# RWKV-7 and mLSTM stages of a hybrid encoder layer: decay as diagonal matrices, state copies on ScalarE, coefficients by rows, products ordered by tile shape

## The chip, the core and the metric

The kernel runs on one core of a Trainium2 chip. The metric is the device time of one execution in microseconds. TensorE is called PE here, VectorE DVE, ScalarE ACT, GpSimd POOL, SyncE SP; SP, and sometimes ACT, only start DMAs.

## What is computed

One layer of an encoder with 1024 positions of width 1024, all in 32-bit floats. A normalised input is projected once to the inputs of four mixers (RWKV-7, mLSTM, RG-LRU, HGRN2) and to four gate blocks; the gated mixer outputs are projected back and a convolutional feed-forward network follows. The shift, scale and gate vectors come from `c` by a projection ("ada"). The change touches the first two mixers, in both directions of time, and the ada projection:

```python
# RWKV-7, 8 heads of 64; S is v x k
S_t = S_{t-1} diag(w_t) + (S_{t-1} a_t) b_t^T + v_t k_t^T ;  y_t = S_t r_t
k_bonus = 0.5 * (kts[0] + kts[1])
bonus = jnp.sum(r_h * k_bonus * r_k, axis=-1, keepdims=True) * v_h
y = (groupnorm(ys[0] + ys[1]) * ln_w + ln_b + bonus) * (sigmoid(xg) @ g2)
# mLSTM, 4 heads: decayed attention inside a chunk plus a matrix state between chunks
```

## The kernel before

Everything is written for one core, with positions in blocks of 128. A scheduler orders the instructions of each engine, by priorities and dependencies; in the RWKV loop PE's order is the order in the code (a manual schedule), and a few instructions are tied to come after a named one.

**The RWKV loop** (`rw_first`, `rw_btm`, `rw_solve`, `rw_second`, `rw_chain`, about L890 to L1165, driven from L1307) makes 16 turns, one for each pair of heads `j` and pair of blocks. A turn handles four chunks of 64 positions for each of two heads and two directions, and three groups of chunks are under way at once: the chain of one, the second half of the preparation of the next, the first half of the one behind that. The gate projections, some 1200 products of 128x512, fill PE between the steps (`pieces`).

- First half: DVE scans the log decays (L863), ACT takes two exps per direction (L865, L867), DVE and POOL build `rw_AR` and `rw_BK` (L877 to L885), PE multiplies them (L915), DVE masks the products (L923). Then 16x16 triangular blocks go through DRAM by DMAs on SP (L971 to L976), ACT copies them (L978) and DVE inverts them by small products and sums (L986 to L999): the solve.
- Second half: `rw_second` joins the small inverses to 64x64 ones in four stages (L1026, L1033, L1046, L1054). `rw_btm` turns `rw_BK` by PE transposes (L956) and copies it to `rw_btm` (L957, ACT).
- Chain: four steps, each L1117 (state `rw_mv` times keys), a copy `rw_s` (L1120, ACT), L1127 (times the inverse), a copy `rw_uv` (L1130, ACT), L1134 (old state by an identity) plus L1142 (update) into one PSUM tile, and L1148 (DVE), which multiplies that tile by the decay of the chunk `rw_gc` and writes the next state `rw_mv`, or `rw_M` behind the last step. The outputs are L1091 and L1096, in two places of the step.

**The epilogue** `rw_post` (L1165) makes 8 blocks of norm, bonus and gate on POOL, DVE and ACT, one product on PE (L1202) and four transposes (L1206). The bonus needs coefficients, one per head and position, that the loop makes with a two-column selector (L931) and ACT keeps (L934). HGRN2 and its projections run beside the epilogue.

**mLSTM** `ml_pair` (L575) makes two heads: state updates (L605, DVE L610), scores (L631), and for each head, direction and chunk the sum of two products, decayed scores times values (L643, contraction 128) and query times state (L644, contraction 64), three chunks to a PSUM bank, copied by ACT (L648). `fill` puts other projections in between. Beside it run sixteen ada pieces: 1 MB of weights each, summed into one tile by DVE (L1382, L1384) and one by POOL (L1391, L1395), then one-column products with ones on PE (L1408).

## Time and profile before

| | us |
|---|---|
| median of 3 runs | 2743.36 |
| lowest, highest | 2740.43, 2747.32 |
| the profiled execution | 2752.19 |
| its span, first to last instruction | 2750.4 |
| PE, DVE, POOL, ACT busy in it | 2539.7, 1781.4, 1178.2, 916.3 |

The order of the stages in the profiled execution: norm, ada and first projections to about 440 us, the RWKV loop to 1050, the epilogue of RWKV beside the projections of HGRN2 to 1180, HGRN2 to 1500, mLSTM to 1750, then branch outputs and feed-forward network. In the rows below times are microseconds from the start of the span, unless marked ns.

### The profile page before, as it was taken

To read this page: it belongs to the slowest core of one execution; us is meant where nothing else is said; L and a number is where in the kernel's file an instruction comes from. 1 tells how busy PE (TensorE), PEld (TensorE's weight loads), DVE (VectorE), ACT (ScalarE), POOL (GpSimd) and SP (SyncE) were. 2 spreads that over 40 slices of the span, in tenths; PEclk is the share of its full clock that TensorE was granted. 3 is DMA by queue.
4 is the path that set the end of the run, shared out by engine and by line. 5 is a ranking of instruction groups with operands and counts; after the bars stand their busy time and mean duration, and the time that the engine had idled before them with its cause. 6 is when DMAs were issued, how large, how long until landed. Compare 5 with 4: busy or idle time off the path is not lost. (4 is left out here: it accounts for less than half of the span.)

```text
span 2750.4 us, 46997 instructions
## 1 busy us (share of the span) xinstructions
PE 2539.7 (92%) x18625; PEld 2032.3 (74%) x18625; DVE 1781.4 (65%) x2868; ACT 916.3 (33%) x1653; POOL 1178.2 (43%) x1164
## 2 busy tenths in 40 slices
PE   5999888999999999799989999999998999999998
PEld 4777666676776777587778767788776888887887
DVE  7567765676667733754553675367479998896345
ACT  4355532333333322433332232111234444342002
POOL 3654462443344315632212443367456444445332
PEclk9999998999999999999989988999999999999999
DMA  6422253444444324311111544554542222216222
GB/s 214 130 70 65 89 153 79 115 108 111 105 106 113 95 72 132 88 44 41 47 32 36 154 132 140 184 189 156 174 121 88 92 83 79 85 57 202 83 80 77
DMA packets 402117, 290.25 MB, mean 106 GB/s; under 512 B 121258, under 2 KB 364248, under 8 KB 401896
## 3 DMA queue, kind: packets, MB, share of 16 engines
q1 hardware_dynamic: 362920, 247.85, 31.1%
q10 hardware_dynamic: 38976, 39.40, 4.3%
q8 instruction: 146, 2.39, 0.4%
q14 instruction: 75, 0.61, 0.1%
HBM read 223.40 MB, written 63.77 MB: 104 GB/s over the span
## 5 line engine op out<-in xcount | busy, mean ns | idle before, releaser
L119 POOL TENSOR_TENSOR w_lo<-w_raw,w_hi 128x512 fp32r<-128x512 f32 x284 | 393.2, 1385 | 780.9 <-DVE w_hi L118 277.7
L125 PE MATMUL pbig<-uh,w_hi 128*128 128x512 f32 x1208 | 508.2, 422 | 23.4 <-ACT w_hi L116 8.5
L127 PE MATMUL pbig<-uh,w_lo 128*128 128x512 f32 x1208 | 485.3, 403 | 6.7 <-POOL w_lo L119 6.6
L126 PE MATMUL pbig<-ul,w_hi 128*128 128x512 f32 x1184 | 477.0, 403 | 0.0
L125 PEld LDWEIGHTS pbig<-uh,w_hi 128*128 128x128 f32 x1208 | 233.3, 193 | 91.0 <-ACT gt L1230 17.4
L127 PEld LDWEIGHTS pbig<-uh,w_lo 128*128 128x128 f32 x1208 | 233.4, 194 | 62.0 <-POOL w_lo L119 10.8
L126 PEld LDWEIGHTS pbig<-ul,w_hi 128*128 128x128 f32 x1184 | 229.6, 194 | 42.0 <-issue 1.3
L118 DVE CAST w_hi<-w_raw 128x512 fp32r<-128x512 f32 x224 | 134.0, 599 | 144.9 <-PE pbig L126 82.6
L127 PE MATMUL ppc<-uh,w_lo 128*128 128x512 f32 x340 | 135.6, 402 | 2.6 <-POOL w_lo L119 2.2
L125 PE MATMUL ppc<-uh,w_hi 128*128 128x512 f32 x340 | 134.5, 400 | 1.2 <-DVE w_hi L118 1.2
L126 PE MATMUL ppc<-ul,w_hi 128*128 128x512 f32 x320 | 127.8, 400 | 0.0
L125 PE MATMUL ppa<-uh,w_hi 128*128 128x512 f32 x220 | 87.2, 397 | 5.5 <-DVE w_hi L118 5.4
L127 PE MATMUL ppa<-uh,w_lo 128*128 128x512 f32 x220 | 86.9, 395 | 0.8 <-POOL w_lo L119 0.8
L127 PE MATMUL ppy<-uh,w_lo 128*128 128x512 f32 x216 | 85.3, 395 | 1.1 <-POOL w_lo L119 1.1
L125 PE MATMUL ppy<-uh,w_hi 128*128 128x512 f32 x216 | 85.8, 397 | 0.1
L1833 ACT CAST w_hi<-s 128x512 fp32r<-128x512 f32 x84 | 52.1, 620 | 97.3 <-PE ppc L126 22.4
L126 PE MATMUL ppa<-ul,w_hi 128*128 128x512 f32 x208 | 84.1, 404 | 0.0
L126 PE MATMUL ppy<-ul,w_hi 128*128 128x512 f32 x208 | 82.7, 398 | 0.0
L127 PEld LDWEIGHTS ppc<-uh,w_lo 128*128 128x128 f32 x340 | 65.8, 194 | 17.9 <-POOL w_lo L119 2.6
L125 PEld LDWEIGHTS ppc<-uh,w_hi 128*128 128x128 f32 x340 | 65.3, 192 | 16.5 <-DVE w_hi L118 2.1
L1384 DVE SCALAR_TENSOR_TENSOR ada_acc<-ada_w,sc,ada_acc 128x256 f32<-128x256 f32 x112 | 73.1, 655 | 2.0
L204 ACT CAST uh<-h_raw 128x1024 fp32r<-128x1024 f32 x22 | 23.0, 1052 | 151.9 <-PE ppc L127 123.8
(789 smaller groups left out, 6319.1 us busy)
## 6 DMA issues: line engine op xcount, KB each, us to landing
w_raw<-in_w_in_dram SPq DMA_DIRECT2D x172, 256.0 KB
ada_w<-in_ada_w_dram SPq DMA_DIRECT2D x24, 1024.0 KB
s_raw<-in_ffn_up_dram SPq DMA_DIRECT2D x84, 256.0 KB
dG<-gt ACTq DMA_DIRECT2D x64, 256.0 KB
sgt<-dG SPq DMA_DIRECT2D x32, 512.0 KB
rw_in<-dIn SPq DMA_DIRECT2D x32, 384.0 KB
w_raw<-in_ffn_down_dram SPq DMA_DIRECT2D x44, 256.0 KB
dF<-cv SPq DMA_DIRECT2D x22, 512.0 KB
```

The lines of the kernel that those rows point to most:

```text
L118: nc.vector.tensor_copy(out=hi, in_=raw[:, k0:k0 + m])
L119: nc.gpsimd.tensor_tensor(lo, raw[:, k0:k0 + m], hi.bitcast(F32), op=SUB)
L125: nc.tensor.matmul(pt, lhsT=wh, rhs=uh, start=start, stop=False)
L126: nc.tensor.matmul(pt, lhsT=wh, rhs=ul, start=False, stop=False)
L127: nc.tensor.matmul(pt, lhsT=wl, rhs=uh, start=False, stop=stop)
L204: nc.scalar.copy(hi, src)
L1384: nc.vector.scalar_tensor_tensor(acc, w[:, k, :], self.sc[:, k:k + 1], acc, op0=MUL, op1=ADD)
L1833: nc.scalar.copy(hi, x)
```

## The change

1. **Chain.** For each turn POOL makes 64x64 diagonal matrices `dg` out of the decays (L960 of the new kernel). The old state is multiplied by them on PE (four products in place of two by an identity), and `rw_btm` is built as a product of `rw_BK` with `dg` in place of a transpose, so that the PSUM tile holds the decayed state at once. ACT copies it (L1153) where DVE multiplied it.
2. **Outputs.** The products for y of a step stand in one place, those of one tile shape together.
3. **Coefficients.** The selector becomes the weight and the data stream past it, which gives rows of 256 positions; ACT copies them, SP writes them to DRAM (`dC`), and the epilogue loads, adds and transposes them (L1183).
4. **Order of the loop.** The first three stages of `rw_second` move one place to the back; the solve stands in the code behind the first step of the next turn.
5. **mLSTM.** The two kinds of products are grouped by bank, two chunks to a bank, and `MF` and the rate of the filler follow. **ada**: POOL adds the two partial sums, so that PE makes one product where it made two.

```diff
@@ -568,7 +568,7 @@
     SEQ = "q0 p0 q1 a32 o0 p1 o1"
-    MF = (2, 1, 2)
+    MF = (2, 2, 2)
@@ -634,18 +634,21 @@
                 num = self.t(wp, [P, NCK, 129], f"ml_num{d}")
-                for g in range(0, NCK, 3):
-                    n = min(3, NCK - g)
-                    pt = self.ps([P, 512])
-                    for i in range(n):
-                        c = g + i
-                        o = pt[:, 129 * i:129 * i + 129]
-                        nc.tensor.matmul(o, lhsT=D[d][:, c, :], rhs=v[:, c, h, :], start=True, stop=False)
-                        mm = nc.tensor.matmul(o, lhsT=Qd[d][r, c * P:(c + 1) * P], rhs=St[d][r, c, :],
-                                              start=False, stop=True)
+                for gs in ((0, 2), (4, 6)):
+                    pts = [self.ps([P, 512]) for _ in gs]
+                    for i in range(2):
+                        for x in ((0, 1), (1, 0))[i]:
+                            for g, pt in zip(gs, pts):
+                                c, o = g + i, pt[:, 129 * i:129 * i + 129]
+                                l, rr = ((D[d][:, c, :], v[:, c, h, :]) if x == 0 else
+                                         (Qd[d][r, c * P:(c + 1) * P], St[d][r, c, :]))
+                                mm = nc.tensor.matmul(o, lhsT=l, rhs=rr, start=(x == i), stop=(x != i))
...
                     self.fill(mm, self.MF[1])
-                    nc.scalar.copy(num[:, g:g + n, :], pt[:, :129 * n].rearrange("p (n v) -> p n v", v=129))
+                    for g, pt in zip(gs, pts):
+                        nc.scalar.copy(num[:, g:g + 2, :], pt[:, :258].rearrange("p (n v) -> p n v", v=129))
@@ -700,11 +703,12 @@
             nc.gpsimd.memset(x, 0.0)
+        self.rw_e64 = self.t(wp, [P, 64], "rw_e64")
+        nc.vector.tensor_tensor(self.rw_e64, self.ident[:, 0:64], self.ident[:, 64:P], op=ADD)
...
         z = self.rw_TFt[0].rearrange("p d m t -> p (d m t)")
-        self.last_pm = None
@@ -925,13 +929,14 @@
             yield
-        pt = self.ps([P, 2, NB, 2], self.pat())
+        pt = self.ps([P, 2, P * NB], self.pat())
         for d in range(2):
-            for n in range(NB):
-                nc.tensor.matmul(pt[:, d, n, :], lhsT=ops[d][2][:, P * n:P * n + P], rhs=self.rw_sel[:, j, :],
-                                 start=True, stop=True)
+            nc.tensor.matmul(pt[0:2, d, :], lhsT=self.rw_sel[:, j, :], rhs=ops[d][2], start=True, stop=True)
         for d in range(2):
-            nc.scalar.copy(self.rw_coef[:, d, n0[d]:n0[d] + NB, 2 * j:2 * j + 2], pt[:, d])
+            cf = self.t(wp, [2, P * NB], "rw_tmp", bufs=3)
+            nc.scalar.copy(cf, pt[0:2, d, :])
+            nc.sync.dma_start(out=self.dC[2 * j:2 * j + 2, d, P * n0[d]:P * (n0[d] + NB)], in_=cf)
@@ -949,12 +954,20 @@
+        dg = b["dg"] = self.t(wp, [P, 2, NC, 64], "rw_dg", bufs=2)
+        nc.gpsimd.tensor_tensor(dg, self.rw_e64.unsqueeze(1).to_broadcast([P, 2 * NC, 64]).rearrange(
+            "p (d c) k -> p d c k", d=2), b["gc"].unsqueeze(3).to_broadcast([P, 2, NC, 64]), op=MUL)
+        pts = [self.ps([P, 2, NC, 64], self.pat()) for h in range(2)]
         for d in range(2):
-            bk = b["bk"][d]
-            pt = self.ps([P, NC, P], self.pat())
             for c in range(NC):
-                nc.tensor.transpose(pt[:, c, :], bk[:, c, :, :], self.ident)
-            nc.scalar.copy(btm[:, d], pt)
+                for h in range(2):
+                    hr = slice(64 * h, 64 * h + 64)
+                    nc.tensor.matmul(pts[h][:, d, c, :], lhsT=b["bk"][d][hr, c, :, :], rhs=dg[hr, d, c, :],
+                                     start=True, stop=True)
+        for h in range(2):
+            nc.scalar.copy(btm[:, :, :, 64 * h:64 * h + 64], pts[h])
@@ -1045,7 +1058,7 @@
                                  start=True, stop=True, tile_position=(32 * q0, 32 * q1))
-        E3 = self.t(wp, [P, NC, 32], "rw_E3")
+        E3 = self.t(wp, [P, NC, 32], "rw_E")
@@ -1079,28 +1092,21 @@
-        def y(st, part):
+        def y(st):
             cs = (st, NC - 1 - st)
-            if st % 2 == 0 and part == 0:
+            if st % 2 == 0:
...
-            def y2(d, start):
+            for d, c in enumerate(cs):
                 for h, hr, _ in halves:
-                    nc.tensor.matmul(py[hr, st % 2, d, :], lhsT=b["cb"][hr, d, cs[d], 64:P], rhs=b["uv"][hr, d, cs[d], h, :],
-                                     start=start, stop=not start, tile_position=(64 * h, 64 * h))
-            def y1(d, start):
+                    nc.tensor.matmul(py[hr, st % 2, d, :], lhsT=b["cb"][hr, d, c, 64:P], rhs=b["uv"][hr, d, c, h, :],
+                                     start=(d == 0), stop=True, tile_position=(64 * h, 64 * h), skip_group_check=True)
+            for d, c in enumerate(cs):
                 for h, hr, _ in halves:
-                    nc.tensor.matmul(py[hr, st % 2, d, :], lhsT=b["ar"][d][:, cs[d], 1, h, :], rhs=b["mv"][:, d, cs[d], h, :],
-                                     start=start, stop=not start, tile_position=(0, 64 * h))
-            if part == 0:
-                y2(0, True)
-                y1(0, False)
-                y1(1, True)
-                return
-            y2(1, False)
+                    nc.tensor.matmul(py[hr, st % 2, d, :], lhsT=b["ar"][d][:, c, 1, h, :], rhs=b["mv"][:, d, c, h, :],
+                                     start=False, stop=True, tile_position=(0, 64 * h), skip_group_check=True)
@@ -1114,9 +1120,10 @@
                     for h, hr, _ in halves:
-                        nc.tensor.matmul(pt[hr, d, :], lhsT=b["ar"][d][:, c, 0, h, :], rhs=b["mv"][:, d, c, h, :],
-                                         start=True, stop=True, tile_position=(0, 64 * h))
-                s = self.t(wp, [P, 2, 64], "rw_s", bufs=2)
+                        self.last_s = nc.tensor.matmul(pt[hr, d, :], lhsT=b["ar"][d][:, c, 0, h, :],
+                                                       rhs=b["mv"][:, d, c, h, :], start=True, stop=True,
+                                                       tile_position=(0, 64 * h))
+                s = self.t(wp, [P, 2, 64], "rw_s")
@@ -1130,27 +1137,22 @@
                 pm = self.ps([P, 2, 64], "pc")
-                for h, hr, _ in halves:
-                    nc.tensor.matmul(pm[hr], lhsT=self.ident[hr, hr], rhs=both(b["mv"], st, h, hr), start=True, stop=True,
-                                     tile_position=(64 * h, 64 * h))
+                for d, c in enumerate(cs):
+                    for h, hr, _ in halves:
+                        nc.tensor.matmul(pm[hr, d, :], lhsT=b["dg"][hr, d, c, :], rhs=b["mv"][hr, d, c, h, :],
+                                         start=(d == 0), stop=True, tile_position=(64 * h, 64 * h), skip_group_check=True)
             if st:
-                y(st - 1, 0)
+                y(st - 1)
...
                     for h, hr, _ in halves:
-                        self.last_pm = nc.tensor.matmul(pm[hr, d, :], lhsT=b["btm"][:, d, c, hr], rhs=b["uv"][:, d, c, h, :], start=False,
+                        nc.tensor.matmul(pm[hr, d, :], lhsT=b["btm"][:, d, c, hr], rhs=b["uv"][:, d, c, h, :], start=False,
...
                 for h, hr, _ in halves:
-                    g = b["gc"][hr, 0, st:st + 1]
-                    g = bass.AP(g.tensor, g.offset, [list(g.ap[0]), [2 * (NC - st) - 1, 2], [0, 64]])
-                    mo = M[j][hr, :, h, :] if st == NC - 1 else both(b["mv"], st + 1, h, hr)
-                    nc.vector.tensor_tensor(mo, pm[hr], g, op=MUL)
-            if st:
-                y(st - 1, 1)
+                    nc.scalar.copy(M[j][hr, :, h, :] if st == NC - 1 else both(b["mv"], st + 1, h, hr), pm[hr])
             if st == NC - 1:
-                y(st, 0)
-                y(st, 1)
+                y(st)
@@ -1173,7 +1175,13 @@
         coef = self.t(wp, [P, NT, 8], "ro_coef")
-        nc.vector.tensor_tensor(coef, self.rw_coef[:, 0], self.rw_coef[:, 1], op=ADD)
+        cf = self.t(wp, [8, 2, T], "ro_cf")
+        nc.sync.dma_start(out=cf, in_=self.dC)
+        nc.vector.tensor_tensor(cf[:, 0], cf[:, 0], cf[:, 1], op=ADD)
+        pt = self.ps([P, NT, 8], "pc")
+        for n in range(NT):
+            nc.tensor.transpose(pt[:, n, :], cf[:, 0, P * n:P * n + P], self.ident[:8, :8])
+        nc.scalar.copy(coef, pt)
@@ -1274,7 +1282,7 @@
         self.dSG = self.t(dr, [P, T], "dSG")
-        self.rw_coef = self.t(self.cp, [P, 2, NT, 8], "rw_coef")
+        self.dC = self.t(dr, [8, 2, T], "dC")
@@ -1314,7 +1322,10 @@
                     next(chn, None)
-                    if st > 1:
+                    if st == 0 and g > 0:
+                        with self.tc.issue_after(self.last_s.ins):
+                            next(pend, None)
+                    if st == 3:
@@ -1327,6 +1338,8 @@
                         next(fst, None)
+                        if st == 3:
+                            next(sec, None)
@@ -1341,8 +1354,7 @@
                             lin = self.rw_lin(*order[g + 2], wp)
-                        with self.tc.issue_after(self.last_pm.ins) if self.last_pm is not None else ExitStack():
-                            next(fst, None)
+                        pend = fst
@@ -1395,7 +1407,9 @@
             if pend is None:
-                self.ada_end([(g, accs)], "pa", G)
+                if ks < 8:
+                    nc.gpsimd.tensor_tensor(acc, acc, accs[0], op=ADD)
+                self.ada_end([(g, [acc])], "pa", G)
@@ -1640,7 +1654,7 @@
                         self.filler = self.gates(dG, g0, 32 - self.NE)
-                        self.rate = 8.0 * (32 - self.NE - g0) / (4 * self.MF[0] + 12 * self.MF[1] + 6 * self.MF[2])
+                        self.rate = 8.0 * (32 - self.NE - g0) / (4 * self.MF[0] + 8 * self.MF[1] + 6 * self.MF[2])
```

The new lines move the instructions of an engine as follows. First ACT in the first step of a turn: `rw_s`, `rw_uv` and `rw_mv` are the chain's, `rw_tmp` and `rw_l` belong to the exps of the next group. Before (L865 and L867 are the exps, L957 copies `rw_btm`):

```order
L865 ACTIVATE rw_l_1520_9673<-rw_tmp_9779 128x256
L957 COPY rw_btm_9761<-ppt_9762 128x512
L867 ACTIVATE rw_tmp_9779<-rw_tmp_9779 128x256
L957 COPY rw_btm_9761<-ppa_9768 128x512
L865 ACTIVATE rw_l_1523_9682<-rw_tmp_9804 128x256
L867 ACTIVATE rw_tmp_9804<-rw_tmp_9804 128x256
L1120 COPY rw_s_9861<-ppc_9856 128x128
```

No copy of the state stands among them. In the changed kernel (L869 and L871 are the exps, L970 copies `rw_btm`):

```order
L1137 COPY rw_uv_8911<-ppc_9450 64x2x64 x2
L869 ACTIVATE rw_l_1488_9384<-rw_tmp_9500 128x256
L871 ACTIVATE rw_tmp_9500<-rw_tmp_9500 128x256
L869 ACTIVATE rw_l_1491_9393<-rw_tmp_9525 128x256
L871 ACTIVATE rw_tmp_9525<-rw_tmp_9525 128x256
L970 COPY rw_btm_9472<-ppa_9475 128x8x64
L970 COPY rw_btm_9472<-ppt_9476 128x8x64
L1153 COPY rw_mv_8916<-ppc_9457 64x2x64 x2
L1127 COPY rw_s_9570<-ppc_9565 128x128
```

The copies of `rw_btm` stood among the exps; now they stand behind all four, and the copy of the state, which was DVE's, stands behind them. On DVE before, the state stood here, behind both scans (L863) in the first step of a turn:

```order
L863 SCALAR_TENSOR_TENSOR rw_tmp_9779<-rwrs_717,rw_l_1520_9673 128x256
L883 SCALAR_TENSOR_TENSOR rw_tmp_9792<-rw_l_1521_9675,rw_in_9776 128x256
L877 TENSOR_TENSOR rw_AR_9783<-rw_in_9776,rw_l_1520_9673 64x4x63
L879 TENSOR_TENSOR rw_AR_9783<-rw_in_9776,rw_l_1520_9673 64x4x64
L877 TENSOR_TENSOR rw_AR_9783<-rw_in_9776,rw_l_1520_9673 64x4x63
L879 TENSOR_TENSOR rw_AR_9783<-rw_in_9776,rw_l_1520_9673 64x4x64
L863 SCALAR_TENSOR_TENSOR rw_tmp_9804<-rwrs_717,rw_l_1523_9682 128x256
L1148 TENSOR_TENSOR rw_mv_9229<-ppc_9748,rw_gc_8717 64x2x64 x2
L885 SCALAR_TENSOR_TENSOR rw_BK_9784<-rw_tmp_9792,rw_tmp_9779 64x4x64 x2
```

That row is gone from DVE in the changed kernel; the rest stands there as before.

On PE in the epilogue, one of the eight blocks before (L1206 the transposes of a block, L1202 the product of the next, the rest projections of HGRN2's input):

```order
L126 MATMUL pbig_11880<-ul_24_94,w_hi_11875 128x512
L127 MATMUL pbig_11880<-uh_16_86,w_lo_11876 128x512
L1206 MATMUL ppc_11510<-ident_73,ro_y_1766_11484 128x128 x4
L1202 MATMUL ppc_11541<-ro_1754_11442,ro_sg_11446 128x512
L125 MATMUL pbig_11879<-uh_17_87,w_hi_11875 128x512
L126 MATMUL pbig_11879<-ul_25_95,w_hi_11875 128x512
L127 MATMUL pbig_11879<-uh_17_87,w_lo_11876 128x512
```

Projections stand on both sides of the block. From the end of the projections on in the changed kernel, where L1214 and L1210 are the same two, PE has:

```order
L125 MATMUL ppy_12150<-uh_18_88,w_hi_12145 128x512
L126 MATMUL ppy_12150<-ul_26_96,w_hi_12145 128x512
L127 MATMUL ppy_12150<-uh_18_88,w_lo_12146 128x512
L1214 MATMUL ppc_11810<-ident_73,ro_y_1808_11784 128x128 x4
L1210 MATMUL ppc_11841<-ro_1803_11764,ro_sg_11768 128x512
L1214 MATMUL ppc_11844<-ident_73,ro_y_1817_11818 128x128 x4
```

All eight blocks follow one another there in this way; before, 16 to 70 rows of other products stood between two of them. On PE in mLSTM, from the end of one bank to the next (`pps`, `ppt`) before:

```order
L643 MATMUL pps_15870<-ml_v_11726,ml_D_2371_15816 128x129
L644 MATMUL pps_15870<-ml_S_2352_15686,ml_q_2350_15682 128x129
L643 MATMUL ppt_15878<-ml_v_11726,ml_D_2371_15816 128x129
L644 MATMUL ppt_15878<-ml_S_2352_15686,ml_q_2350_15682 128x129
L643 MATMUL ppt_15878<-ml_v_11726,ml_D_2371_15816 128x129
```

The kinds alternate, within a bank and from one to the next. One bank in the changed kernel (L647 is both kinds, told apart by `ml_D` and `ml_S`), with the projections that follow:

```order
L647 MATMUL ppt_16095<-ml_v_12060,ml_D_2407_16046 128x129
L647 MATMUL ppt_16095<-ml_S_2396_15987,ml_q_2394_15983 128x129 x2
L647 MATMUL ppt_16095<-ml_v_12060,ml_D_2407_16046 128x129
L126 MATMUL pbig_16759<-ul_19_89,w_hi_16748 128x512
L127 MATMUL pbig_16759<-uh_11_81,w_lo_16749 128x512
```

A bank's two products with the state now stand side by side, between two with the decayed scores.

## Rows read from the trace of the kernel before

**Rows 1.** The page: engines' busy time; costliest group (busy, mean ns, idle, releaser).

```profile
PE 2539.7 (92%) x18625; PEld 2032.3 (74%) x18625; DVE 1781.4 (65%) x2868; ACT 916.3 (33%) x1653; POOL 1178.2 (43%) x1164
...
L119 POOL TENSOR_TENSOR w_lo<-w_raw,w_hi 128x512 fp32r<-128x512 f32 x284 | 393.2, 1385 | 780.9 <-DVE w_hi L118 277.7
```

**Rows 2.** Windows by stage: stretch, its us, busy us (instructions) per engine, PEclk, DMA, GB/s.

```profile
440.00:1050.00 610.00, 565.18 (x7663) 434.51 (x7663) 391.19 (x979) 207.92 (x565) 224.23 (x358) 0.97 0.40 101
1060.00:1180.00 120.00, 101.93 (x730) 78.59 (x729) 80.17 (x119) 47.19 (x65) 80.03 (x59) 0.94 0.38 107
1510.00:1750.00 240.00, 225.28 (x1096) 174.07 (x1094) 148.73 (x259) 65.10 (x136) 96.17 (x89) 0.89 0.45 140
1608.00:1636.00 28.00, 24.57 (x94) 18.30 (x94) 18.97 (x28) 13.42 (x28) 13.31 (x12) 0.52 0.39 128
```

**Rows 3.** Waits of PE, 440 to 1050: waiter, releaser, total us, times, longest.

```profile
PE ppc L1117 <- DVE rw_mv L1148: 28.7, 17, 3.1
```

**Rows 4.** Timeline of one turn: start us, duration us, engine, line, output<-inputs, count, wait.

```profile
758.16 0.67 DVE L863 TENSOR_TENSOR_SCAN rw_tmp<-rwrs,rw_l 128x256 f32<-128x256 bf16 x1
...
758.87 0.42 ACT L865 ACTIVATE rw_l<-rw_tmp 128x256 f32<-128x256 f32 x1 [2.96 <-DVE rw_tmp L863]
...
759.19 0.57 ACT L957 COPY rw_btm<-ppt 128x512 f32<-128x512 f32 x1
...
761.74 0.69 DVE L863 TENSOR_TENSOR_SCAN rw_tmp<-rwrs,rw_l 128x256 f32<-128x256 bf16 x1
...
762.46 0.61 DVE L1148 TENSOR_TENSOR rw_mv<-ppc,rw_gc 64x128 f32<-64x128 f32 x2
...
762.80 0.77 PE L1117 MATMUL ppc<-rw_mv,rw_AR 128*64 128x64 f32 x8 [2.83 <-DVE rw_mv L1148]
...
772.70 0.45 PE L1026 MATMUL pps<-rw_RT,rw_cb 32*32 32x32 f32 x32
...
772.98 0.48 PE L1026 MATMUL pps<-rw_R,rw_cb 32*32 32x32 f32 x32
...
776.84 0.27 PE L915 MATMUL ppt<-rw_AR,rw_BK 64*128 64x128 f32 x1
...
776.95 0.27 PE L915 MATMUL ppt<-rw_AR,rw_BK 64*128 64x128 f32 x1
...
786.00 0.62 ACT L978 COPY rw_SB<-rw_pr 32x256 f32<-32x256 f32 x1 [0.57 <-DMA rw_pr<-dA]
...
795.92 0.68 DVE L863 TENSOR_TENSOR_SCAN rw_tmp<-rwrs,rw_l 128x256 f32<-128x256 bf16 x1
...
799.83 0.33 PE L1117 MATMUL ppc<-rw_mv,rw_AR 128*64 128x64 f32 x2 [0.73 <-DVE rw_mv L1148]
...
809.01 0.77 PE L1117 MATMUL ppc<-rw_mv,rw_AR 128*64 128x64 f32 x8 [1.05 <-DVE rw_mv L1148]
```

**Rows 5.** Lines L1148 and L1130: duration ns min/median/max, first and last start.

```profile
L1148 DVE TENSOR_TENSOR rw_mv<-ppc,rw_gc x96: 270/288/296, 450.9 to 1039.5; 64x128 f32<-64x128 f32 x96
...
L1130 ACT COPY rw_uv<-ppc x128: 242/260/263, 447.1 to 1048.1; 64x128 f32<-64x128 f32 x128
```

**Rows 6.** Window of the epilogue, tile ro_y alone; then timeline rows of one block.

```profile
1060.00:1175.00 115.00, 5.92 (x32) 4.10 (x32) 26.96 (x32) 5.06 (x8) 55.03 (x40) 0.94 0.38 106
...
1096.70 1.29 POOL L1187 TENSOR_TENSOR ro_y<-ro_y,ro_y 128x512 f32<-128x512 f32 x1 [5.06 <-DMA ro_y<-dYr]
...
1110.30 0.63 PE L1206 MATMUL ppc<-ident,ro_y 128*128 128x128 f32 x4
```

**Rows 7.** Timeline of PE in mLSTM: columns as in Rows 4.

```profile
1590.15 1.16 PE L631 MATMUL ppt<-ml_qT,ml_kT 64*128 64x128 f32 x8
...
1602.00 0.49 PE L644 MATMUL ppt<-ml_S,ml_q 64*128 64x129 f32 x2
...
1606.18 0.49 PE L644 MATMUL pps<-ml_S,ml_q 64*128 64x129 f32 x2
...
1606.59 1.05 PE L1408 MATMUL ppa<-ones,ada_acc 128*128 128x1 f32 x8
```

## The prediction

> **What bounds the kernel now.** I read the page first: TensorE is busy for 92% of the span, the others for far less [rows 1]. So time comes out only where TensorE stands still, runs at a low granted clock, or has fewer or cheaper instructions. The table by stage then shows which of these holds where the change lies [rows 2]. From 440 to 1050 us (the RWKV chain) PE is idle for 610.0 - 565.2 = 44.8 us; from 1060 to 1180 (the RWKV epilogue with the HGRN2 projections) for 18.1 us at clock 0.94; from 1510 to 1750 (mLSTM) for 14.7 us, but at clock 0.89, and from 1608 to 1636 at 0.52, that is, almost wholly on the lower of the two levels, 1.2 GHz. The chain waits mainly at one place, L1117 on the state that DVE writes in L1148: 28.7 us in 17 waits [rows 3].
>
> Why the state is late is seen in one turn [rows 4]. A turn is a loop: the scan that ends the solve starts at 758.16; L1117 of step 1 at 762.80 (4.64 later, after a wait of 2.83); the last L915 at 776.95 (ends 777.22, 14.42 after L1117); the copy of the solve's input at 786.00; the next scan at 795.92; its L1117 at 799.83 (3.91 later). The loop takes 37.8 us from scan to scan. DVE is in order, so the state at 762.46 stands behind both scans, which follow the solve. The wait is thus an end of a loop through PE, DVE, DMAs and ACT; taking the multiplication off DVE doesn't remove the loop.
>
> **Part 1: chain.** L1148 leaves DVE: 128 pairs of 0.288 us by the rows of its two tiles (96 of them in the row shown). ACT gets as many copies of the same shape, priced by L1130's 0.260 [rows 5]. The change of engine alone is worth nothing; the queue counts. On ACT the copy of step 1 stands behind two exps of each direction and both btm copies (excerpt of ScalarE in the part on the change). The second exp needs the second scan. In a turn like the first one shown, where four DVE operations part the scans, the second scan ends at 761.74 + 0.69 = 762.43; then come exp 0.42, exp 0.42 (partly overlapped; 0.8 together), two btm copies 1.14 and the state 0.52: 764.9 or 6.7 after the scan, less 0.15 for copies that overlap, so 6.55 against 4.64. In a turn of the other kind the second scan starts 1.25 after the first: 1.25 + 0.69 + 0.8 + 1.14 + 0.52 - 0.05 = 4.35 against 3.91. Mean of both: +1.2 us per turn. At the later steps the state copy follows uv directly.
>
> Against it, from L1117 to the end of L915 (14.42): the wait of step 2 in every other turn (1.05 [rows 4]) goes, since nothing of DVE stands ahead of the copy: -0.5; the first stage of rw_second (L1026, its two groups from 772.70 to 773.46, some 0.7 without the tail [rows 4]) moves one place back, behind L915: -0.7; y grouped by tile shape: -0.15 before L915; the low clock after the longer waits: -0.3. Together -1.65. In the solve DVE loses the two M updates (0.58) and gains the E3 copy (about 0.3): -0.3. A turn: +1.2 - 1.65 - 0.3 = -0.75. Over 15 turns -11, with 16 turns' rest **-12 us**. The ends: if every L1117 wait goes and the clock (0.97 over 610 us) gains the larger part of what it lacks, -28.7 - 11 = -40; if the ACT queue holds the state in every turn as in the first kind (+2.3) and PE gains nothing, +20.
>
> The rest of this part is small. Eight transposes of 128 columns per turn, 0.9 us by L915's spacing of 0.11 (776.84 to 776.95), become 16 products of 64 columns in two passes, 32 records: at best half of L1026's 64 records on small tiles side by side, 0.35, at worst 16 times L915's 0.11 for each pair, 1.75 [rows 4]. That is -0.55 to +0.85 us of PE a turn, -9 to +14 in all, off the loop; I take 0, near the middle, and keep the ends inside those above. The diagonals are one GpSimd operation per turn, 1.385 by L119's row of the same width [rows 1], two places ahead of its readers: hidden. Coefficients: 8 two-column products of L931 become 2 of 256 columns: no change within 0.1 us per turn. Grouping y saves the turn of the array to another tile shape twice a step, of which some 0.3 us per turn lies outside the loop, filled by gate products.
>
> The Trainium skill speaks against the move of the copies: ScalarE: Activation LUTs, Rules for kernel authors, wants plain multiplications on VectorE and budgets some 0.3 us plus 0.83 ns per element for ScalarE; for 128 elements that is an estimate of 0.41 us per copy. The rows have 0.260 for just this shape, so the trace disagrees; by the page the two copies of a step would cost 0.3 more, three times a turn on the loop, and the part would come to about 0 instead of a gain.
>
> **Part 2: epilogue.** rw_post's eight blocks each end in four transposes on PE. Before, 16 to 70 rows of other products stand between two blocks. Now 47 products stand between the first gate product and the first transposes, and from there all eight blocks follow with nothing between (excerpt of TensorE). PE can't run ahead of the slowest engine that feeds them. GpSimd has 40 operations on ro_y, 55.03 us [rows 6], so 6.9 us a block; the latency of one block, from its first sum at 1096.70 to its transposes at 1110.30, is 13.6 us [rows 6]. With blocks overlapped by GpSimd's pace the last ends some 60 to 65 us after the first sum; PE is busy for the first 15 (47 products by about 0.23, and what stands ahead), and the blocks themselves have about 8. Idle: 63 - 15 - 8 = 40, less 2 that the next weights hide: 38. Before, the stretch lost 18.1 idle and 0.06 x 120 = 7.2 of clock: 25 [rows 2]. **+13 us**, between 0 (GpSimd, with its weight halves no longer among them, runs closer) and +61 (each block waits for the last, below). The displaced projections run elsewhere; they aren't lost.
>
> **Part 3: mLSTM and ada.** 64 D products and 64 state products alternate, each a change from a 128-row to a 64-row tile. From 1602.00 to 1606.18 ten of them start, 0.418 each; L631's four of one shape take 1.16 with the tail of a 0.27 record, so 0.25 each [rows 7]. Now a bank of four has the order D, state, state, D (excerpt): 64 changes fewer, by 0.16: **-10 us**. From 1608 to 1636 PE is busy for 24.57 us at clock 0.52 [rows 2], so about 12 us went to the lower level; it begins right behind this alternating run, and half of that I count: **-6**. The added eight evacuations lie beside PE: ACT has 65 of 240 us there [rows 2]. In ada, 64 one-column records go, by 1.05 less a tail of 0.25 for 7 gaps, 0.114: **-7**; GpSimd's 16 additions have room (96 of 240 us), and DVE's sums feed them earlier than PE needs them. Together **-23**; ends -38 (full clock) and -8 (DVE's state updates, which L605 and L644 need, become late).
>
> **The sum.** The profiled execution took 2752.2 us (2750.4 of it span), 8.8 above the median of 2743.4. 2752.2 - 12 + 13 - 23 = 2730; less 8.8 against the median: **2721**.
>
> **Rivals.** (a) *The waits at L1117 truly go* (-40), since in turns of the second kind the state needs no DVE and the slack passes on; for it: 17 waits have this one releaser. Against: the loop. 2752.2 - 40 + 13 - 23 = 2702, 2693 against the median; with the epilogue at 0, 2680. (b) *The state queues on ACT*: the loop is longer in the first kind, and in the second too since btm's copies wait for products on the new diagonals, +2.3 - 1.65 = +0.65 per turn, +10; 2752.2 + 10 + 13 - 23 = 2752, 2743: no change. For it: the order of ACT; against: half the turns have early scans. (c) *Slower: the epilogue goes block by block.* If each block's loads and sums start only when the tile of the one ahead is free, the cadence is the 13.6 us of one block: 8 x 13.6 - 15 - 8 = 86 idle against 25, +61; 2752.2 - 12 + 61 - 23 = 2778, 2769. The time is over the old one from a cadence of about 10 us ((25 + 35 + 15 + 8)/8 = 10.4). For it: one wait of GpSimd on a ro_y load of 5.06 us [rows 6], and yb's single buffer; against: GpSimd's other work leaves its queue. That the change doesn't do what it says can be left out for the order, whose rows show it; for the time it is (b), where the work changes its engine and the wait only its releaser.
>
> **How the numbers follow.** Forecast 0.50, (a) 0.16, (b) 0.17, (c) 0.17. A measurement here tells 0.3%, 8.2 us. Faster: forecast and (a), 0.66; within: 0.17; slower: 0.17. The forecast's own range is 2695 to 2740. The range reaches down to (a) with its further end, 2680, and up to 2756, halfway to (c): about 0.2 is left out.
>
> **What would show it.** Right: waits at L1117 of a few us in half the turns, now released by ACT; PE idle of 35 to 45 us in the epilogue, GpSimd busy throughout; L647's products at 0.33 on average and the mLSTM stage some 20 us shorter at a clock over 0.92. Wrong: a loop over 38.5 us; an epilogue cadence over 10 us; a mLSTM stage that shrinks by less than 10, with PE waiting for ml_wk or ada sums.

## The result, and the profile after

| | before | after |
|---|---|---|
| median of the runs made side by side | 2744.59 (4 runs) | 2778.46 (4 runs, 2774.18 to 2781.44) |
| ratio, 95% interval | | 1.0124 [1.0104, 1.0143] |
| profiled execution | 2752.19 | 2774.18 |
| last L377 of HGRN2 starts at | 1415.7 | 1451.1 |

The kernel became 34 us slower; the forecast was 22 faster. The page of after answers to [rows 1]: PE has hardly more to do than before, so the 22 us by which the two profiled executions differ (2750.4 and 2772.4 us of span) are time in which PE stands still.

```profile
PE 2541.3 (92%) x19145; PEld 2032.6 (73%) x19145; DVE 1726.0 (62%) x2741; ACT 942.1 (34%) x1779; POOL 1208.6 (44%) x1196
```

The table by stage (columns as in [rows 2]) shows where. mLSTM stands later in after, its first product with `ml_D` by 34 us and its last by 18, so that the stretch that answers to 1510:1750 is the last row:

```profile
440.00:1050.00 610.00, 571.11 (x8118) 439.04 (x8119) 344.14 (x838) 241.38 (x680) 237.76 (x366) 0.96 0.39 101
1060.00:1180.00 120.00, 76.28 (x292) 55.29 (x292) 49.84 (x84) 21.30 (x39) 66.54 (x54) 0.76 0.36 102
1544.00:1768.00 224.00, 200.18 (x1038) 160.64 (x1037) 142.82 (x260) 66.28 (x144) 112.83 (x106) 0.90 0.49 153
```

In the epilogue PE's idle time went from 18.1 to 43.7 us and the granted clock from 0.94 to 0.76, which the forecast had nearly right for the idle time and not at all for the clock. And DVE and ACT do far less there than before (49.84 against 80.17, 21.30 against 47.19): work of HGRN2 that stood in this stretch has left it. In the chain PE is busier, at a lower clock (0.96 against 0.97). The waits of PE in the chain (440 to 1060), and then in the epilogue (1060 to 1180), answer to [rows 3]:

```profile
PE pps L1067 <- DVE rw_E L1062: 18.5, 11, 3.4
PE ppc L1150 <- ACT rw_uv L1137: 13.4, 7, 3.1
...
PE ppc L1214 <- DVE ro_y L1211: 40.7, 8, 13.0
```

The wait for the state (28.7 us in [rows 3]) is gone from the list, as rival (a) had it. Two others of about the same sum stand in its place. Neither is a wait for the state: L1067 is the last stage of `rw_second`, L1150 the update by `uv`.

### The profile page after: what moved, and what is told of

Read it like the earlier page. It is cut to its first block, busy times and chain, and to the rows that moved or that the text cites. A ratio compares the mean times of both kernels' runs of the same rounds, so it can differ in the third digit from the quotient of the medians.

```text
span 2772.4 us, 48190 instructions
## 1 busy us (share of the span) xinstructions
PE 2541.3 (92%) x19145; PEld 2032.6 (73%) x19145; DVE 1726.0 (62%) x2741; ACT 942.1 (34%) x1779; POOL 1208.6 (44%) x1196
## 5 line engine op out<-in xcount | busy, mean ns | idle before, releaser
L116 ACT CAST w_hi<-w_raw 128x512 fp32r<-128x512 f32 x60 | 37.0, 617 | 121.9 <-PE pbig L126 102.8
```

Of the source, the lines that this page charges most:

```text
L116: nc.scalar.copy(hi, raw[:, k0:k0 + m])
```

## The experiments

All ratios are against runs of the kernel before on the same chip in the same batch, with 95% intervals; its medians there lay between 2743.4 and 2745.0. Where two experiments are compared with each other, the difference is that of their medians, from different batches; by the ratios it comes out up to some 5 us otherwise.

**1. The 8 KB alone.** The kernel before, with the change's new tile `ro_cf` (8 KB in each partition's address range) set to zero in the epilogue's pool and never read. Apart from that one operation on DVE, no arithmetic and no order of the code is touched.

```diff
         coef = self.t(wp, [P, NT, 8], "ro_coef")
+        cf = self.t(wp, [8, 2, T], "ro_cf")
+        nc.vector.memset(cf, 0.0)
```

> The kernel before, plus one scratch tile of 8 KB per partition in the pool of the RWKV epilogue, set to zero once and read by nobody; nothing of the change is in it. Theory S (space: the 8 KB that the coefficient rows take in the epilogue's pool, and not their arithmetic or DMAs, push the eight epilogue blocks together on PE, and PE then waits for them): about 25 us slower than before, PE waiting some 40 us at the epilogue's transposes between 1080 and 1150 us. Rival A (the added loads, sum and transposes of the coefficients make the epilogue late): no change, within 8 us.

Measured: 2774.76, ratio 1.0108 [1.0083, 1.0133], +30 us. The tile alone does it, without the change's arithmetic and DMAs. PE's wait in the epilogue is that of after (the same product under another line number), and the wait for the state in the chain is as before:

```profile
PE ppc L1117 <- DVE rw_mv L1148: 28.4, 18, 3.1
...
PE ppc L1208 <- DVE ro_y L1205: 39.4, 8, 12.5
```

How the space acts is seen on ACT. In the kernel before, the first evacuation of HGRN2's projections starts at the beginning of the epilogue:

```profile
1068.65 0.60 ACT L1547 ACTIVATE hg_in<-pbig 128x512 f32<-128x512 f32 x1
```

In after it comes right behind the last block's copy of the epilogue:

```profile
1142.57 0.59 ACT L1216 COPY ro_yT<-ppc 128x512 f32<-128x512 f32 x1 [3.49 <-PE ppc L1214]
...
1144.88 1.09 ACT L1561 ACTIVATE hg_in<-pbig 128x512 f32<-128x512 f32 x2
```

and so it does in the experiment (L1549, first at 1137.44, behind the last block's copy at 1135.1). On SP's queue HGRN2's first load (`hgm`) stands at 1060.59 before, among the loads of the blocks, and at 1127.27 in after, behind the last of them:

```profile
1060.59 0.45 SPq L1537 DMA_DIRECT2D hgm<-in_k_hgm_dram  x1
...
1127.27 0.42 SPq L1551 DMA_DIRECT2D hgm<-in_k_hgm_dram  x1
```

The first row is of before, the second of after. In the kernel of experiment 2, whose tile is small, the load is back among those of the blocks:

```profile
1065.46 0.43 SPq L1551 DMA_DIRECT2D hgm<-in_k_hgm_dram  x1
```

The reading that fits all of this is that HGRN2's tiles no longer find room beside the epilogue's, so its stage begins only when the epilogue's space is given back. The allocator's addresses are not in the profile, so that this is argued; shown is that the tile is the cause (the two slow kernels share nothing else of the change in this stage: one sets it to zero, the other loads it), and that its size decides (experiment 2).

**2. The changed kernel with a small tile.** The same coefficients by rows, but 1 KB in the address range: 64 partitions, eight DMAs and one transpose in place of one DMA and eight transposes.

```diff
-        cf = self.t(wp, [8, 2, T], "ro_cf")
-        nc.sync.dma_start(out=cf, in_=self.dC)
+        cf = self.t(wp, [8 * NT, 2, P], "ro_cf")
+        for n in range(NT):
+            nc.sync.dma_start(out=cf[8 * n:8 * n + 8], in_=self.dC[:, :, P * n:P * n + P])
...
-        for n in range(NT):
-            nc.tensor.transpose(pt[:, n, :], cf[:, 0, P * n:P * n + P], self.ident[:8, :8])
+        nc.tensor.transpose(pt.rearrange("p n h -> p (n h)"), cf[:, 0], self.ident[:8 * NT, :8 * NT])
```

> The changed kernel, with the coefficients loaded as 64 rows of 128 positions (1 KB per partition instead of 8, one transpose instead of eight). Theory S: the epilogue's waits fall from 40.7 us to about 15, and the kernel is 20 to 28 us faster than the changed one, about 2752, some 0.3% over the kernel before. Rival A: the loads from DRAM are still there (eight of them), so no more than 5 us are gained.

Measured: 2741.88, 0.9993 [0.9977, 1.0009]. That is 36.6 us off the changed kernel's time, more than the 20 to 28 expected. In the epilogue PE waits 8.2 us for `ro_y`, at clock 0.93:

```profile
PE ppc L1214 <- DVE ro_y L1211: 8.2, 4, 5.8
```

**3. Coefficients alone.** The kernel before with the coefficients by rows in the small tile, nothing else.

> The kernel before with the coefficients by rows, in the small tile; nothing else of the change. Part 1 of the prediction: no change within 0.1 us per turn, so within 3 us of the kernel before (2744). Rival (the copies and DMAs of the rows stand ahead of others on ACT and SP): 5 to 15 us slower.

Measured: 2745.78, 1.0002 [0.9990, 1.0013]. The rows are worth nothing and cost nothing; only their tile cost.

**4. The parts outside RWKV.** The kernel before with the mLSTM part, and with mLSTM and ada (both as in the change's diff).

> The kernel before with the mLSTM part alone, without ada's addition. Prediction's terms: 10 for the tile shapes and 6 for the clock, so 16 faster (2728); ada's 7 would then be missing from the 13.6 us that both gave together. If ada gives nothing because its products lie beside waits, this run equals both together, 2731; if ada gives its 7, it is about 2738.

> The kernel before with the mLSTM and ada parts of the change alone. The prediction's part 3 says 23 us faster (2721). What the two traces show from the start of mLSTM to the start of the feed-forward network says 11 us (2733).

Measured: 2738.76, 0.9982 [0.9967, 0.9997] for mLSTM alone, -5 us; 2730.9, 0.9948 [0.9930, 0.9966] for both, -13.6, so ada is worth some 9. The tile changes went as reckoned. In the second of these kernels a bank of four starts as follows, 1647.10 to 1648.46, 0.34 for each product:

```profile
1647.10 0.47 PE L647 MATMUL ppt<-ml_v,ml_D 128*128 128x129 f32 x2
1647.50 0.71 PE L647 MATMUL ppt<-ml_S,ml_q 64*128 64x129 f32 x4
1648.14 0.49 PE L647 MATMUL ppt<-ml_v,ml_D 128*128 128x129 f32 x2
1648.46 0.39 PE L647 MATMUL pps<-ml_v,ml_D 128*128 128x129 f32 x2
```

The clock is another matter. Over the whole stage it is hardly higher, first before, then this kernel:

```profile
1500.00:1750.00 250.00, 235.28 (x1140) 182.34 (x1139) 156.28 (x263) 68.45 (x139) 97.41 (x90) 0.89 0.44 136
...
1490.00:1726.00 236.00, 215.01 (x1107) 174.66 (x1106) 154.79 (x265) 72.36 (x149) 117.97 (x107) 0.91 0.49 152
```

But it falls at another place. Before, it falls at 1607.7, within a run of alternating products, and PE doesn't wait ahead of the fall or behind it:

```profile
1592.00:1608.00 16.00, 15.87 (x82) 12.17 (x81) 14.80 (x21) 4.81 (x12) 9.62 (x8) 0.99 0.41 132
1608.00:1624.00 16.00, 16.00 (x51) 11.68 (x50) 8.76 (x14) 2.65 (x5) 4.76 (x6) 0.50 0.56 179
```

In the second kernel of this experiment it falls at 1589.0, during a wait of 4.4 us ahead of a product of L647:

```profile
1584.00:1592.00 8.00, 3.62 (x19) 3.00 (x17) 4.38 (x7) 2.49 (x9) 8.00 (x6) 0.81 0.40 131
1592.00:1608.00 16.00, 16.00 (x59) 13.28 (x60) 13.81 (x23) 3.58 (x8) 9.40 (x10) 0.50 0.49 148
```

The profile names no releaser for that wait. It ends 0.1 us behind the operation on DVE that writes `ml_D` (L634, 1588.43 to 1589.12), which itself waited for ACT, and ACT for POOL. The four other falls of before between the first and the last product with `ml_D` (1577, 1662, 1700, 1713) also come without a wait of PE beside them; this kernel has only one other, at a wait too. So the falls within the alternating runs went, and a wait brought one of its own. With mLSTM alone one fall without a wait is left (1670), so that the grouping and ada's fewer products are not told apart.

**5. The order of the loop.** From experiment 2, the order of the RWKV loop as before: the stages of `rw_second` and the last piece of the solve go back to their places. Then only the stages go back.

```diff
-                    if st == 0 and g > 0:
-                        with self.tc.issue_after(self.last_s.ins):
-                            next(pend, None)
-                    if st == 3:
+                    if st > 1:
                         next(sec, None)
...
-                        if st == 3:
-                            next(sec, None)
...
-                        pend = fst
+                        with self.tc.issue_after(self.last_pm.ins) if self.last_pm is not None else ExitStack():
+                            next(fst, None)
```

> The changed kernel with the small coefficient tile and with the order of the RWKV loop as it was before (stages of rw_second one place earlier, the solve's last piece at the end of the turn); the diagonals, the copies on ACT, the grouped outputs stay. Theory E (the new wait of PE for the copy of rw_E, which stands on DVE behind the start of the solve, is what took the place of the wait for the state): that wait, 18.5 us, goes, and the loop takes 38.3 us per turn instead of 39.6, so 12 to 18 us faster than the run with the small tile alone. Rival P (the loop is longer by the dearer products for rw_btm, 1.07 us per turn, and by PE work in general): no more than 4 us.

> The changed kernel with the small coefficient tile and with one half of the loop's order as before: the stages of rw_second stand one place earlier again, the solve's last piece stays where the change put it. Theory E (the stages' move is the harmful half: with it the copy of rw_E stands behind the start of the solve on DVE): the time of the run with the whole old order, 2716 to 2726; PE's wait for rw_E gone. Rival: the place of the solve is the harmful half; then about 2742, as with the small tile alone.

Measured: 2720.07, 0.9917 [0.9892, 0.9942] for the whole old order, 21.8 less than experiment 2; 2723.52, 0.9920 [0.9891, 0.9948] for the stages alone. So the move of the stages is what costs (18 to 22 us), and the place of the solve in the code is worth nothing that these runs can tell. The reason stands on DVE. Before, the copy behind the third stage (L1049, the input of the last) starts 3.70 us ahead of the solve's first operation:

```profile
782.95 0.29 DVE L1049 COPY rw_E<-pps 128x128 f32<-128x128 f32 x1 [1.44 <-PE pps L1046]
...
786.65 0.17 DVE L986 COPY rw_ST<-rw_SB 64x8 f32<-64x8 f32 x1 [3.41 <-ACT rw_SB L978]
```

In after the stages lie one place later, and the copy (L1062) stands on DVE behind the first operations of the solve, which wait for a DMA and an ACT copy. PE's last stage waits with it:

```profile
787.23 0.62 ACT L991 COPY rw_SB<-rw_pr 32x256 f32<-32x256 f32 x1 [3.83 <-DMA rw_pr<-dA]
787.88 0.17 DVE L999 COPY rw_ST<-rw_SB 64x8 f32<-64x8 f32 x1 [6.25 <-ACT rw_SB L991]
...
789.04 0.27 DVE L1062 COPY rw_E<-pps 128x128 f32<-128x128 f32 x1
...
789.36 0.45 PE L1067 MATMUL pps<-rw_R,rw_E 32*32 32x32 f32 x32 [3.44 <-DVE rw_E L1062]
```

With the stages back, both new waits are nearly gone, and the wait for the state returns, now released by ACT. The first list is of the kernel with the stages alone back, the second of that with the whole old order:

```profile
PE pbig L125 <- ACT gt L1238: 9.8, 13, 1.0
PE ppc L1123 <- ACT rw_mv L1153: 8.8, 8, 2.5
...
PE ppc L1150 <- ACT rw_uv L1137: 1.7, 2, 1.5
```

```profile
PE ppc L1124 <- ACT rw_mv L1154: 13.6, 10, 2.4
```

One wait has grown: that for `gt`, the copies of the gate projections on ACT. It was 5.9 us in the kernel before and 0.9 in after. ACT now has the state's copies too; that these are the reason was not tried.

**6. Who writes the state.** From the kernel with the old order, first the copies on DVE (the diagonals stay), then no diagonals at all (decay by DVE, `rw_btm` by transposes, as before).

```diff
-                    nc.scalar.copy(M[j][hr, :, h, :] if st == NC - 1 else both(b["mv"], st + 1, h, hr), pm[hr])
+                    nc.vector.tensor_copy(out=M[j][hr, :, h, :] if st == NC - 1 else both(b["mv"], st + 1, h, hr), in_=pm[hr])
```

> The run with the old order of the loop and the small coefficient tile, with the state's copies on DVE instead of ACT (the diagonals stay). Theory D (the state late on DVE, behind the solve and the scans, was worth something): PE's waits at the first product of a step rise from 13.6 us to 25 or more and the time by 8 to 15 us, to about 2732. Rival (the engine of the copy is worth nothing, as the prediction had it: the loop through the solve stays): within 5 us of 2720.

> The run with the old order and the small coefficient tile, without the diagonals: the decay is multiplied on DVE while the state is evacuated, rw_btm comes from PE transposes, as before; grouped outputs, coefficient rows, mLSTM and ada stay. If the diagonals with ACT's copies pay (theory D), 2728 or more. If their dearer products for rw_btm (1.07 us a turn more) eat what the shorter wait gives, 2715 to 2725.

Measured: 2814.08, 1.0247 [1.0223, 1.0270] with the copies on DVE, 94 us more than on ACT where 8 to 15 were expected; 2756.15, 1.0045 [1.0030, 1.0061] without diagonals, 36 more. PE's wait for the state in the two:

```profile
PE ppc L1124 <- DVE rw_mv L1154: 83.4, 14, 7.4
```

```profile
PE ppc L1114 <- DVE rw_mv L1146: 47.0, 17, 4.4
```

The 94 are not the price of the engine alone. Both kernels write the state on DVE, and yet the one with diagonals is 58 us slower. Its copy stands later in DVE's order: 5.96 us behind the start of the second scan in a turn like the first of [rows 4], where the other kernel's multiplication stands right behind that scan:

```profile
709.67 0.69 DVE L868 TENSOR_TENSOR_SCAN rw_tmp<-rwrs,rw_l 128x256 f32<-128x256 bf16 x1
...
715.63 0.61 DVE L1154 COPY rw_mv<-ppc 64x128 f32<-64x128 f32 x2
```

```profile
768.17 0.69 DVE L866 TENSOR_TENSOR_SCAN rw_tmp<-rwrs,rw_l 128x256 f32<-128x256 bf16 x1
768.90 0.61 DVE L1146 TENSOR_TENSOR rw_mv<-ppc,rw_gc 64x128 f32<-64x128 f32 x2
```

How much of the 58 us is this place, and how much the diagonals' own products, was not tried.

**7. The products for y.** From the old order, y in two places of the step as before, with diagonals; then the same without diagonals.

```diff
-                y(st - 1)
+                y(st - 1, 0)
...
+            if st:
+                y(st - 1, 1)
```

> The run with the old order of the loop and the small coefficient tile, with the output products in two places of a step as before. By the two traces, the grouped ones cost 0.34 us less per turn on PE; if a turn is bound by PE's work, this run is 5 us slower than that one, 2725; if by the loop, within 2.

> The run without the diagonals, with the output products in two places of a step as before: what is left of the change is mLSTM, ada, the coefficient rows in the small tile, and small buffers. If the parts add up (mLSTM with ada -13.6, coefficients 0), 2731. Then the diagonals with ACT's copies are worth 2731 - 2712 = 19 with the outputs in two places, and the 36 that they gave with grouped outputs hold a second cost, of grouping while the state is on DVE. If it is near 2756, grouping is innocent and the diagonals are worth the 36.

Measured: 2711.74, 0.9871 [0.9855, 0.9888] with diagonals and 2730.37, 0.9958 [0.9943, 0.9974] without. The first was expected to be 5 us slower than its partner, or within 2 of it; it is 8 faster. Grouping y costs 26 us where DVE writes the state (2756.15 - 2730.37), and the turns of the loop show it: they take 40.4 us grouped and 38.9 in two places. Where ACT writes the state, it is 8 us by the medians (2720.07 - 2711.74), but the turns are not longer for it (37.8 grouped, 38.0 in two places), and the same pair in experiment 8 differs by 3 us at equal ratios: a cost is not shown there. The pair of this experiment gives the cleanest price of the diagonals with the copies on ACT: 19 us gained (24 by the ratios).

```profile
PE ppc L1131 <- ACT rw_mv L1161: 6.3, 6, 1.8
```

```profile
PE ppc L1121 <- DVE rw_mv L1153: 33.2, 19, 3.0
```

**8. What stands ahead of the state on ACT.** From the old order, the two `rw_btm` copies are issued behind the state's copy of the first step; then the four exps too; then, from the first of these, y in two places.

```diff
+                    if st == 0:
+                        with (self.tc.issue_after(self.last_mv.ins) if prev is not None else ExitStack()):
+                            next(bt, None)
```

> The run with the old order of the loop and the small coefficient tile, with one order more: ACT's two copies of rw_btm come behind the state's copy of the first step instead of ahead of it. Theory Q (the state of the first step is late in ACT's queue, 13.6 us of PE's waits, in good part for these two copies of 0.57 us): about half of the waits go, 5 to 8 us faster than that run, 2713. Rival (what is late is the exps, which wait for the scans on DVE): within 3 us.

> As the run before, and the exps of the next group too come behind the state's copy of the first step. Theory Q: no wait of PE for the state is left, and the time falls by 13 us in all against the run with the old order, 2707. Rival L (the exps lie on the loop through the solve, and their delay comes back as a later solve): no faster than the run before, or slower.

> Both improvements at once: the copies of rw_btm behind the state's copy (-10) and the outputs in two places (-8), on the run with the old order and the small coefficient tile (2720). If both take from the same waits for the state (6.5 and 6.3 us left by each of 13.6), 2706 to 2711; if they add, 2702.

Measured: 2710.09, 0.9870 [0.9852, 0.9889] with the copies moved, 10 less than without, and the wait for the state falls from 13.6 to 6.5; 2778.32, 1.0119 [1.0102, 1.0137] with the exps moved as well, where 2707 was expected: what they feed becomes late, as its rival had it, and PE waits 40 us for `rw_BK` instead:

```profile
PE ppa L920 <- DVE rw_BK L890: 20.6, 7, 3.9
PE ppt L920 <- DVE rw_BK L890: 19.8, 7, 4.2
```

With y in two places 2707.48, 0.9870 [0.9852, 0.9887]. That is the lowest median of the kernels tried, 36 us less than before and 71 less than the change as given; by its ratio it is not told apart from the two kernels with one of the moves (0.9870 and 0.9871). The wait for the state is down to 1.0, and the longest that is left is that for `gt`:

```profile
PE pbig L125 <- ACT gt L1251: 11.0, 10, 1.3
PE ppt L920 <- DVE rw_BK L890: 3.7, 6, 0.9
...
PE ppc L1133 <- ACT rw_mv L1163: 1.0, 2, 0.7
```

The length of a turn, from the first to the sixteenth copy of the solve's input on ACT (one line in each kernel, 15 turns), orders the kernels of experiments 5 to 8 as their times do, but for one pair: the old order and the kernel with y in two places (experiment 7), 8 us apart the other way. Before, after, these two and the fastest:

```profile
L978 ACT COPY rw_SB<-rw_pr x16: 618/622/642, 392.0 to 979.7; 32x256 f32<-32x256 f32 x16
...
L991 ACT COPY rw_SB<-rw_pr x16: 618/620/624, 389.9 to 982.8; 32x256 f32<-32x256 f32 x16
...
L992 ACT COPY rw_SB<-rw_pr x16: 619/622/640, 392.5 to 959.1; 32x256 f32<-32x256 f32 x16
...
L992 ACT COPY rw_SB<-rw_pr x16: 619/622/635, 390.7 to 960.0; 32x256 f32<-32x256 f32 x16
...
L994 ACT COPY rw_SB<-rw_pr x16: 618/622/640, 390.4 to 950.8; 32x256 f32<-32x256 f32 x16
```

A turn is 39.2, 39.5, 37.8, 38.0 and 37.4 us. The kernels of experiments 1 and 4 and that of experiment 3 keep the loop's order of before, and theirs are 38.8 to 39.3, so that less than half a us of a turn tells nothing.

## Why the prediction was wrong, point by point

| term | forecast | measured | from |
|---|---|---|---|
| chain | -12 | +12, within 7 | ratios of experiments 2 and 4: (0.9993 - 0.9948) x 2744 |
| epilogue | +13 | +37 | after less experiment 2; the tile alone +30 |
| mLSTM and ada | -23 | -14 | experiment 4 |
| sum | -22 | +35 | the result: +34 |

**The chain: the sign was wrong, in two steps that cancel partly.** The working had "the change of engine alone is worth nothing; the queue counts" and "taking the multiplication off DVE doesn't remove the loop". The first holds for the durations: two copies to the last state took 0.52 us in after, 0.26 each, as [rows 5] had it. The second failed: the diagonals with the copies on ACT gain 19 us (experiment 7), and a turn falls from 38.9 to 38.0 us. The loop was real, but I took the state's place behind the scans as part of it; a state on ACT does not stand behind the solve and the scans on DVE, and the loop gets shorter. Rival (a) was the better mechanism here, at about half its price. What decided is the in-order queue in which the operation stands, not its time (0.288 us on DVE, 0.260 on ACT). The Trainium skill (ScalarE: Activation LUTs, Rules for kernel authors) gives multiplications to VectorE, for its time per element in bf16. In these runs, in 32 bits, following that for the state would have cost the 19 us. The loop of 37.8 us was read from one turn; over fifteen it is 39.2 in the kernel before, so that the sign "a loop over 38.5 us" held before the change already.

The step that turned the gain into a loss is "the first stage of rw_second [...] moves one place back, behind L915: -0.7". I counted its time on PE and nothing of its copies on DVE. Three stages moved, and the copy behind the third came to stand behind the solve. I had priced that copy at 0.3 us of DVE time in the solve; it is a wait of PE of 18.5 us in 11 turns, with 13.4 for `uv` beside it. The move costs 18 us (experiment 2 against the stages back, 2741.88 - 2723.52), and the whole order 22. In the two traces the fifteen turns of after are 5 us longer than those of before, which is within what like loops differ by; the +12 are from the times. "y grouped by tile shape: -0.15" is not borne out either: with the state on ACT the grouping costs something between nothing and 8 us, with the state on DVE 26. The runs do not say by what: the y products of a step now stand in one row ahead of the update's products, while half of them stood behind these, in the time of the state's copy. That this cover was lost fits a cost that is larger where the state is later; it was not tried by itself.

Right were the mechanism of rival (b), the two `rw_btm` copies ahead of the state on ACT: it is 10 us of experiment 8, though its net was not "no change"; coefficients at nothing (experiment 3); and the worst end for the `rw_btm` products. They take 1.73 us from the first to the last in the turn shown, where I put 1.75 as the worst and took the middle:

```profile
797.79 0.32 PE L967 MATMUL ppa<-rw_dg,rw_BK 64*128 64x64 f32 x1
...
799.52 0.27 PE L967 MATMUL ppt<-rw_dg,rw_BK 64*128 64x64 f32 x1
```

That is 0.11 for each pair of records of 64 columns, the spacing of L915's pairs of 128 columns in [rows 4]: half the columns did not make a pair cheaper.

By parts from before: -5 (mLSTM), -9 (ada), 0 (coefficients), +33 (the tile, 30 and 37 in the two tests), -19 (diagonals on ACT), +8 (y), +22 (order), +30 in all; measured +34. The last three are steps along one row of kernels, from 2730.37 to 2741.88, and add up by themselves; measured from two sides are only the start of that row (2730.9 from the kernel before, 2730.37 from the changed one) and the tile.

**The epilogue: the right symptom, another cause.** I saw in the order of TensorE that the blocks would follow in a row, and took this for an effect of the order of the code. It is one of the new tile: experiment 1 shows it with no product moved in the code. The sum had no term for the tile; it put the coefficients at nothing. The pace was near, though GpSimd, which was to set it, was busy for 66.54 of the 120 us and not throughout: from the first block's copy at 1086.3 to the eighth's at 1142.6 the cadence is 8.0 us (forecast 6.9, rival (c) 13.6), and the idle time 43.7 (forecast 38).

```profile
L1216 ACT COPY ro_yT<-ppc x8: 586/586/588, 1086.3 to 1142.6; 128x512 f32<-128x512 f32 x8
```

What failed is the step behind it, "the displaced projections run elsewhere; they aren't lost". Not only projections were displaced but the whole start of HGRN2, with its work on ACT and DVE, and the clock fell to 0.76 in the meantime. So HGRN2 ended 35.4 us later (last L377), of which the chain explains the 3.1 by which its last solve starts later. Rival (c) had the right sign by the wrong mechanism, and its threshold of 10.4 us did not hold: the kernel lost time at a cadence of 8.0.

**mLSTM and ada: right but for the clock.** The products of L643 and L644 took 59.7 us from start to start, those of L647 take 48.7 in after: -11 for a forecast of -10. Ada's one-column products in this stretch took 14.9 and take 7.4, for a forecast of -7. The step that failed is "it begins right behind this alternating run, and half of that I count: -6". The place was read rightly, and the falls of the clock within such runs went; but in the second kernel of experiment 4 the clock falls at a wait of 4.4 us instead, and over the stage it is 0.91 against 0.89. The prediction asked what ends the low clock, and had no term for another wait that would bring one. Of the -11 of the products some 5 arrived, since PE's idle time in the stage rose: from 14.7 us before to 23.8 in after (the row 1544:1768).

## What to carry to other kernels

A tile is a cost even if nothing reads it: before a tile is added to a stage whose successor should overlap it, ask what its bytes per partition leave for that successor, and prefer a shape over many partitions (here 1 KB on 64 in place of 8 KB on 8). When a group of instructions moves on one engine, follow each copy that it feeds on the other engines, which work in order, and ask what that copy now stands behind. A copy moved to a less busy engine may be worth far more than the difference of its durations, if what goes is its place behind a long chain on the old one.

## What the runs showed of the hardware that I had not expected

Grouping products of like tile shape in mLSTM brought each from 0.418 [rows 7] to 0.34 us. The granted clock fell to the lower of its two levels in a stretch in which PE had not waited (15.87 of 16 us busy ahead of the fall, 16.00 behind it), in a run of products of alternating tile shape; in the kernel that groups them no such fall is left, but one at a wait. And an ACT copy of 64x128 from PSUM at 0.26 us, hardly cheaper than DVE's multiplication at 0.288 [rows 5], was worth 19 us in a chain of 16 turns by its place, together with the diagonals that make it a plain copy.
